# More of a modulation's weights loaded ahead, norms in another order, weight units freed earlier, and a branch in other PSUM banks

## The chip, the cores and the metric

The kernel runs on one core of a Trainium2 chip. The metric is the device time of one execution in microseconds (us). A core has five engines that run side by side, each through its own queue in order: TensorE (PE, matrix products; its loads of the fixed operand are PEld), VectorE (DVE), ScalarE (ACT), GpSimd (POOL) and SyncE (SP, which here only issues DMAs). Products are accumulated in banks of PSUM; all else lies in SBUF.

## What is computed

Two blocks, one behind the other, over 256 tokens of width 1024. The first has two layers of a mixer (four branches with gates) and a feed-forward, dense in layer 0 and a mixture of eight experts in layer 1, each behind a layer norm. The second has two layers of attention (two kinds side by side) and a dense feed-forward; its RMS norms and residuals are modulated by rows that come from the conditioning vector `c` through `w_mod`.

```python
def first_block(x, ...):
    for layer in range(DEPTH):                       # DEPTH = 2
        y = mixer_block(x, w_in[layer], ..., w_branch[layer], w_out[layer])
        x = layer_norm(DN_ALPHA * x + y, ln_g[layer, 0], ln_b[layer, 0])
        j = layer // 2
        if layer % 2 == 0:
            y = swiglu(x, ffn_w1[j], ffn_w3[j], ffn_w2[j])
        else:
            y = moe_ffn(x, router_w[j], router_b[j], exp_w1[j], exp_w3[j], exp_w2[j])
        x = layer_norm(DN_ALPHA * x + y, ln_g[layer, 1], ln_b[layer, 1])
    return x

def mixer_block(x, ...):
    ...
    merged = jnp.zeros_like(x)
    for i, (o, w) in enumerate(zip((o_swa, o_rwkv, o_fox, o_dsa), w_rows)):
        merged = merged + gates[:, :, i] * (o @ w)
    return merged @ w_out

def second_block(x, c, ...):
    cond = jax.nn.silu(c)
    for l in range(DEPTH):
        mod = (cond @ w_mod[l] + b_mod[l])[:, None, :]
        sh_a, sc_a, g_a, sh_f, sc_f, g_f = jnp.split(mod, N_MOD, axis=-1)      # N_MOD = 6
        h = rms_norm(x, norm_mix[l]) * (1 + sc_a) + sh_a
        ...                                                                    # attention of h: o_m, o_d
        x = x + g_a * (jnp.concatenate([o_m, o_d], axis=-1) @ w_out[l])
        h = rms_norm(x, norm_ffn[l]) * (1 + sc_f) + sh_f
        x = x + g_f * ((jax.nn.silu(h @ w_gate[l]) * (h @ w_up[l])) @ w_down[l])
    return x
```

## The kernel before

**Products in three parts.** Every large product of f32 operands is made of three PE products of rounded operands: each operand is split into a rounded part (`h`) and the remainder (`l`), and hh, hl and lh are added in PSUM. For weights the class `Stream` does it: `load` issues the DMA of a unit (512 KB, `raw`, L107 on SP) as soon as a `raw` buffer is free (four until the experts, nine from there), `pump` rounds the next unit on ScalarE (`wh`, L125) and emits the remainder of the unit before it on DVE (`wl`, L114). There are six pairs of `wh` and `wl` (`WB`); `W.done()` tells that PE's products with the units taken so far stand in the program, so that their pairs may be used again.

**Who sets the order.** The program is written out by hand, engine by engine, at build time. The main line (stages such as `gates1`, `branch1`, `w_out`, `ln`, `ffn`, `ffn2`, `rms`, `in_2`, each begun by `phase`) emits PE's products and calls `tick` between them; `tick` pumps the weight stream and lets side work (generators: attention chains, the modulation) emit its next piece, when a planner inside the program holds it to be ready by its own costs.

**The modulation** (`mods`) is side work from the first mixer to the second block. The matrix is 2 x 1024 x 6144; each of 24 rows of 512 columns is made of eight steps: SP loads 128 x 512 weights (256 KB, L1694), ScalarE scales them by `c` (L1709), POOL adds them up (L1711, seven of eight); then ScalarE rounds the sum (L1726), POOL makes its remainder (L1728), two PE products with ones add over the partitions, and the row goes to DRAM (L1737). The steps run in the stages that `MODS_IN` names alone. Between a scaling and the next, `ahead` keeps two loads under way (three for some columns), all from one pool of 41 tiles, `b2`.

**Feed-forward** (`ffn`, used three times: once in the first block, twice in the second). 2816 hidden columns in eleven pairs of 128. A pair `p` has 96 PE products of 256 columns for gate and up (in `sm` banks) and 24 of 512 for down (`ffn_down`, into four `acc` banks that stay to the end); down runs one pair behind, and the last two together.

**Projection** (`out_proj`): 96 products of 512 columns into four `acc` banks, for w_out of the mixers and of the second block. Weight units are taken one by one and the last `tail` of them at once, so that the first half of the tokens (t = 0) ends before the second.

**Passage** (`normed_T`): behind a projection or feed-forward, the residual, a norm (`part`, `stats`, `scale`, `shift`: DVE, with one step on POOL) and the transposes of both halves on PE; ScalarE copies the rounded part (`hi`) out of PSUM and DVE the remainder (`lows`, L744 and L750). With `mid`, PE begins the next product on the first half (`nat_start`).

**A mixer's branches**: in the order of `PLAN`, gates and branches; a branch's products go column by column to an `acc` bank, DVE multiplies with the gate (L935) and adds (L936), and in the last branch ScalarE rounds the sum (L940) and DVE makes its remainder (L941) for w_out. Both PSUM rings, `acc` and `sm`, have four banks.

## Time and profile before

| | |
|---|---|
| median of 3 runs (lowest to highest) | 2003.49 us (2001.23 to 2015.73) |
| the profiled execution | 2003.65 us, its span 2001.8 us |
| PE busy | 1832.4 us, 92% of the span |
| PEld, DVE, ACT, POOL busy | 81%, 72%, 58%, 23% |
| mean granted TensorE clock | 0.960 of full speed |
| DMA | 440.08 MB, 220 GB/s on the mean |

The span is the time from the first to the last instruction; outside it lie 1.85 us. Matmuls overlap and their ends are modelled, so a busy PE is not PE at its peak; stages are best compared with a stage that does the same products. The granted clock is the share of full speed (2.4 GHz) that the chip allowed; it is 1.0 or, at 1.2 GHz, 0.5, and a value between is a mean over a stretch.

### The profile page before, as it was taken

To read this page: it belongs to the slowest core of one execution; us is meant where nothing else is said; L and a number is where in the kernel's file an instruction comes from. 1 tells how busy PE (TensorE), PEld (TensorE's weight loads), DVE (VectorE), ACT (ScalarE), POOL (GpSimd) and SP (SyncE) were. 2 spreads that over 40 slices of the span, in tenths; PEclk is the share of its full clock that TensorE was granted. 3 is DMA by queue.
4 is the path that set the end of the run, shared out by engine and by line. 5 is a ranking of instruction groups with operands and counts; after the bars stand their busy time and mean duration, and the time that the engine had idled before them with its cause. 6 is when DMAs were issued, how large, how long until landed. Compare 5 with 4: busy or idle time off the path is not lost. (4 is left out here: it accounts for less than half of the span.)

```text
span 2001.8 us, 31995 instructions
## 1 busy us (share of the span) xinstructions
PE 1832.4 (92%) x11703; PEld 1625.0 (81%) x11703; DVE 1446.5 (72%) x2255; ACT 1170.8 (58%) x1875; POOL 468.0 (23%) x345
## 2 busy tenths in 40 slices
PE   7999987998899999799999999598799888978998
PEld 7899977987698999588888888486698876768998
DVE  5886776666688656788888888777566758857554
ACT  4465744666465564377777777366466655746443
POOL 0110252777530100100000000111246765113000
PEclk9999988999999999889999999798899998989999
DMA  7553575787864444679999999655378785436662
GB/s 218 152 155 106 173 250 186 261 278 243 268 179 140 136 127 137 208 237 334 365 326 352 327 353 354 233 190 161 76 267 281 253 305 191 148 126 210 196 194 95
DMA packets 287071, 440.08 MB, mean 220 GB/s; under 512 B 31764, under 2 KB 178304, under 8 KB 286904
## 3 DMA queue, kind: packets, MB, share of 16 engines
q1 hardware_dynamic: 281960, 428.29, 64.6%
q0 software_dynamic: 2912, 8.59, 1.6%
q8 instruction: 94, 1.54, 0.3%
q10 hardware_dynamic: 2032, 1.06, 0.2%
q14 instruction: 73, 0.60, 0.1%
HBM read 427.60 MB, written 9.75 MB: 218 GB/s over the span
## 5 line engine op out<-in xcount | busy, mean ns | idle before, releaser
L114 DVE TENSOR_TENSOR wl<-raw,wh 128x1024 fp32r<-128x1024 f32 (+2 forms) x694 | 875.9, 1303 | 175.5 <-ACT wh L125 170.5
L125 ACT CAST wh<-raw 128x1024 fp32r<-128x1024 f32 (+2 forms) x694 | 695.4, 1030 | 201.4 <-PE sm L336 61.0
L336 PE MATMUL acc<-wh,b 128*128 128x512 f32 (+1 forms) x1232 | 417.2, 408 | 22.3 <-DVE b L935 10.5
L336 PE MATMUL sm<-b,wh 128*128 128x256 f32 x2112 | 378.1, 283 | 0.9 <-ACT wh L125 0.9
L336 PE MATMUL acc<-b,wh 128*128 128x256 f32 x2048 | 368.2, 283 | 0.2 <-DVE b L416 0.2
L1711 POOL TENSOR_TENSOR b<-b,b 128x512 f32<-128x512 f32 x168 | 309.8, 1844 | 228.5 <-ACT b L1709 215.5
L336 PE MATMUL sm<-wh,b 128*128 128x512 f32 (+1 forms) x1120 | 342.0, 382 | 0.0
L336 PE MATMUL sm<-b,wl 128*128 128x256 f32 x1056 | 302.2, 286 | 38.2 <-DVE wl L114 38.2
L336 PEld LDWEIGHTS sm<-b,wh 128*128 128x128 f32 x2112 | 332.1, 194 | 4.8 <-ACT wh L125 1.4
L336 PEld LDWEIGHTS acc<-b,wh 128*128 128x128 f32 x2048 | 312.5, 189 | 8.7 <-issue 7.3
L336 PEld LDWEIGHTS acc<-wh,b 128*128 128x128 f32 x1232 | 240.5, 196 | 82.2 <-DVE b L935 13.6
L336 PE MATMUL acc<-b,wl 128*128 128x256 f32 x1024 | 286.1, 279 | 3.0 <-DVE wl L114 3.0
L336 PE MATMUL acc<-wl,b 128*128 128x512 f32 (+1 forms) x616 | 248.6, 404 | 4.3 <-DVE wl L114 4.3
L336 PEld LDWEIGHTS sm<-b,wl 128*128 128x128 f32 x1056 | 205.4, 195 | 44.7 <-DVE wl L114 44.6
L336 PEld LDWEIGHTS sm<-wh,b 128*128 128x128 f32 x1120 | 209.8, 189 | 35.0 <-issue 0.2
L1709 ACT ACTIVATE b<-b,ccol 128x512 f32<-128x512 f32 x192 | 137.4, 724 | 151.8 <-DMA b<-in_w_mod_dram 151.8
L336 PE MATMUL sm<-wl,b 128*128 128x512 f32 (+1 forms) x560 | 213.5, 381 | 0.0
L336 PEld LDWEIGHTS acc<-b,wl 128*128 128x128 f32 x1024 | 193.5, 189 | 3.6 <-DVE wl L114 3.6
L336 PEld LDWEIGHTS acc<-wl,b 128*128 128x128 f32 x616 | 120.8, 196 | 30.5 <-DVE wl L114 7.5
L553 POOL TENSOR_TENSOR ln_mv<-ln_mv,mhalf 128x1 f32<-128x1 f32 x8 | 7.5, 932 | 525.4 <-DVE ln_mv L664 525.4
L336 PEld LDWEIGHTS sm<-wl,b 128*128 128x128 f32 x560 | 105.9, 189 | 18.2 <-DVE wl L114 0.5
L340 PE MATMUL sm<-ident,b 128*128 128x128 f32 (+1 forms) x242 | 46.9, 339 | 72.6 <-DVE b L691 32.1
(333 smaller groups left out, 1738.7 us busy)
## 6 DMA issues: line engine op xcount, KB each, us to landing
raw<-in_exp_w_dram SPq DMA_DIRECT2D x216, 512.0 KB
raw<-in_w_in_dram SPq DMA_DIRECT2D x152, 512.0 KB
b<-in_w_mod_dram SPq DMA_DIRECT2D x192, 256.0 KB
raw<-in_ffn_w_dram SPq DMA_DIRECT2D x66, 512.0 KB
raw<-in_exp_w_dram SPq DMA_DIRECT2D x64, 384.0 KB
raw<-in_w_gate_dram SPq DMA_DIRECT2D x44, 512.0 KB
raw<-in_w_up_dram SPq DMA_DIRECT2D x44, 512.0 KB
raw<-in_w_down_dram SPq DMA_DIRECT2D x44, 512.0 KB
```

What stands on the lines that cost most here:

```text
L114: self.K.nc.vector.tensor_sub(*self.lows.pop())
L125: nc.scalar.copy(wh[:, :w], raw[:, :w])
L336: return self.nc.tensor.matmul(out, lhsT, rhs, start=start, stop=stop)
L340: r = self.nc.tensor.transpose(out, in_, ident)
L553: self.nc.gpsimd.tensor_tensor(ap, ap, self.mhalf[:, :n], op=OP.pow)
L1709: nc.scalar.activation(r, r, AF.Copy, scale=cc[:, k : k + 1])
L1711: nc.gpsimd.tensor_add(w["a"], w["a"], r)
```

## The change

**Loads of the modulation.** `MODS_IN` becomes a table of depths: `ahead` keeps as many loads under way as the running stage has there, 9 in the feed-forwards, and `steps` calls it more often. From three pairs before a feed-forward's end the depth is 2 again.

**Units freed ahead.** In `out_proj` and at the end of `ffn`, `W.dn` is moved on and a unit pumped before the last products; the mixers' `tail` is 4 instead of 5.

**Last branch.** Branch 1, the last of a mixer, takes `sm` banks, and the remainder for a column (L941, now L949) is emitted behind the next column's two operations.

**Passages.** `turn` is split into the transposes and `high`; the norm's steps of both halves come ahead of the transposes, the remainders last; the early product `mid` comes behind the second half's `shift`, and at r = 0 there is none.

```diff
-MODS_IN = ("branch3", "gates1", "branch0", "branch1", "w_out", "ffn", "ffn2")
+MODS_IN = {"branch3": 2, "gates1": 2, "branch0": 3, "branch1": 3, "w_out": 4, "ffn": 9, "ffn2": 9}
@@ def phase
         self.main = name
+        self.ahead = MODS_IN.get(name, 2)
@@ def out_proj
-    def out_proj(self, aT, nk, tail=5, split_at=None):
+    def out_proj(self, aT, nk, tail=4, split_at=None):
...
                 if t == 0:
                     self.tick()
+                elif j == tail - 3:
+                    self.W.dn = self.W.ti - 2
+                    self.W.pump()
@@ def normed_T
         if norm:
             part, stats, scale, shift = norm
-            for n in range(2):
-                part(0, n)
-                if early:
-                    scale(0, n)
-            stats(0)
+            for t in range(NT):
+                for n in range(2):
+                    part(t, n)
+                    if early and not t:
+                        scale(t, n)
+                if early and t:
+                    for n in range(2):
+                        scale(t, n)
+                stats(t)
+                if not early:
+                    for n in range(2):
+                        scale(t, n)
+                if not early and t == 0:
+                    for n in range(2):
+                        shift(t, n)
             if early:
-                part(1, 0)
-            else:
                 for n in range(2):
-                    scale(0, n)
-            for n in range(2):
-                shift(0, n)
-        self.turn(xT, src[0], 0, lows[0])
-        if mid:
-            rest = mid(xT)
-        if norm:
-            if early:
-                scale(1, 0)
-            else:
-                part(1, 0)
-            part(1, 1)
...
-        for o in lows[0]:
-            nc.vector.tensor_sub(*o)
+                    shift(0, n)
+        self.high(xT, self.turn(src[0]), 0, lows)
         if norm:
             for n in range(2):
                 shift(1, n)
-        self.turn(xT, src[1], 1, lows[1])
-        for o in lows[1]:
+        if mid:
+            rest = mid(xT)
+        self.high(xT, self.turn(src[1]), 1, lows)
+        for o in lows:
             nc.vector.tensor_sub(*o)
@@ def mixer
-                ps = self.acc().rearrange("p (a b) -> p a b", a=2)
+                ps = (self.acc() if nb < 4 else self.sm()).rearrange("p (a b) -> p a b", a=2)
...
                     nc.scalar.mul(mh[c], mt[c], 0.5)
-                    nc.vector.scalar_tensor_tensor(ml[c], mt[c], 0.5, mh[c], op0=OP.mult, op1=OP.subtract)
-                    del mt[c]
+                    if last:
+                        last()
+
+                    def last(c=c, m=mt.pop(c)):
+                        nc.vector.scalar_tensor_tensor(ml[c], m, 0.5, mh[c], op0=OP.mult, op1=OP.subtract)
@@ def ffn
+            if p == np_ - 3:
+                self.ahead = 2
...
         self.ffn_down(y, hid.pop(np_ - 2), ws[:2], False, False)
+        self.W.dn = self.W.ti - 2
+        self.W.pump()
         self.ffn_down(y, hid.pop(np_ - 1), ws[2:], False, False, True)
@@ def mods
-            while order and len(raws) < (3 if order[0][2] > 2 else 2) and not (self.hold and order[0][2] == 0):
+            while order and len(raws) < self.ahead and not (self.hold and order[0][2] == 0):
...
                 if not raws:
                     ahead()
                     yield AUTO
+                    ahead()
@@ def build
-                xT = self.normed_T(hs, norm, True, self.nat_start(512) if half == 0 else None)
+                xT = self.normed_T(hs, norm, True, self.nat_start(512) if r == 6 else None)
```

How the instructions stand now, at three places. Rows are in program order on one engine; a tile's last number tells buffers apart.

*Second feed-forward, the middle.* SP's loads before, of weights (`raw`) and modulation (`b` from `in_w_mod_dram`):

```order
L107 DMA raw_19622<-in_w_up_dram 128x4x256
L107 DMA raw_19640<-in_w_up_dram 128x4x256
L1694 DMA b_4380_19644<-in_w_mod_dram 128x512
L107 DMA raw_19676<-in_w_down_dram 128x1024
L107 DMA raw_19695<-in_w_down_dram 128x1024
L1694 DMA b_4389_19699<-in_w_mod_dram 128x512
L1694 DMA b_4390_19715<-in_w_mod_dram 128x512
L107 DMA raw_19727<-in_w_gate_dram 128x4x256
L1720 DMA b_4394_19729<-in_b_mod_dram 1x512
L107 DMA raw_19748<-in_w_gate_dram 128x4x256
L1694 DMA b_4399_19751<-in_w_mod_dram 128x512
L1694 DMA b_4400_19753<-in_w_mod_dram 128x512
```

and where ScalarE uses them: L1709 scales, L125 rounds a weight unit.

```order
L1709 ACTIVATE b_4399_19751<-b_4399_19751,ccol_425 128x512
L1333 ACTIVATE b_4406_19805<-sm_19731 128x512
L125 CAST wh_19820<-raw_19573 128x1024
L1726 CAST b_4411_19826<-b_4335_19384 128x512
L1709 ACTIVATE b_4400_19753<-b_4400_19753,ccol_425 128x512
L125 CAST wh_19869<-raw_19622 128x1024
L1709 ACTIVATE b_4401_19769<-b_4401_19769,ccol_425 128x512
```

The load of `b_4400` stands eleven rows behind that of `raw_19622`, and both are used side by side. SP's rows of the change at the same place:

```order
L107 DMA raw_19571<-in_w_gate_dram 128x4x256
L107 DMA raw_19595<-in_w_gate_dram 128x4x256
L1708 DMA b_4385_19610<-in_w_mod_dram 128x512
L1708 DMA b_4386_19626<-in_w_mod_dram 128x512
L107 DMA raw_19644<-in_w_up_dram 128x4x256
L1708 DMA b_4390_19648<-in_w_mod_dram 128x512
L107 DMA raw_19669<-in_w_up_dram 128x4x256
L1708 DMA b_4396_19685<-in_w_mod_dram 128x512
```

and ScalarE's:

```order
L1725 ACTIVATE b_4385_19610<-b_4385_19610,ccol_425 128x512
L125 CAST wh_19809<-raw_19529 128x1024
L1725 ACTIVATE b_4386_19626<-b_4386_19626,ccol_425 128x512
L1725 ACTIVATE b_4390_19648<-b_4390_19648,ccol_425 128x512
L125 CAST wh_19859<-raw_19571 128x1024
L1725 ACTIVATE b_4396_19685<-b_4396_19685,ccol_425 128x512
```

Here `b_4390` is used next to `raw_19571`, and its load stands five rows behind that one's.

*First feed-forward, the beginning.* SP's rows before, where the weights of the second pair and the constants of the next layer (`rows`) are loaded:

```order
L107 DMA raw_3733<-in_ffn_w_dram 128x4x256
L107 DMA raw_3756<-in_ffn_w_dram 128x4x256
L1694 DMA b_695_3763<-in_w_mod_dram 128x512
L1694 DMA b_696_3767<-in_w_mod_dram 128x512
L1737 DMA mod_223<-b_625_3448 1x512
L510 DMA rows_3774<-in_rwkv_mu_dram 8x128
L510 DMA rows_3774<-in_rwkv_w_dram 2x128
L510 DMA rows_3774<-in_rwkv_a_dram 2x128
```

and of the change:

```order
L107 DMA raw_3769<-in_ffn_w_dram 128x4x256
L1708 DMA b_700_3773<-in_w_mod_dram 128x512
L1708 DMA b_701_3775<-in_w_mod_dram 128x512
L1708 DMA b_702_3777<-in_w_mod_dram 128x512
L1708 DMA b_703_3779<-in_w_mod_dram 128x512
L1708 DMA b_704_3781<-in_w_mod_dram 128x512
L1708 DMA b_705_3783<-in_w_mod_dram 128x512
L1708 DMA b_706_3787<-in_w_mod_dram 128x512
L1753 DMA mod_223<-b_621_3427 1x512
L511 DMA rows_3794<-in_rwkv_mu_dram 8x128
L511 DMA rows_3794<-in_rwkv_w_dram 2x128
L511 DMA rows_3794<-in_rwkv_a_dram 2x128
```

Seven loads of the modulation stand in a row now, where two did.

*Layer 0, from the last branch to w_out.* DVE's rows before: L935 and L936 of a column, L941 its remainder, L114 weights:

```order
L935 SCALAR_TENSOR_TENSOR b_550_2970<-b_550_2970,acc_3371 128x512
L936 TENSOR_TENSOR b_393_2144<-b_393_2144,b_550_2970 128x512
L941 SCALAR_TENSOR_TENSOR b_613_3397<-b_393_2144,b_612_3396 128x512
L114 TENSOR_TENSOR wl_3385<-raw_3253,wh_3384 128x1024
L935 SCALAR_TENSOR_TENSOR b_562_3049<-b_562_3049,acc_3400 128x512
L936 TENSOR_TENSOR b_402_2186<-b_402_2186,b_562_3049 128x512
L941 SCALAR_TENSOR_TENSOR b_620_3426<-b_402_2186,b_619_3425 128x512
L114 TENSOR_TENSOR wl_3414<-raw_3293,wh_3413 128x1024
L935 SCALAR_TENSOR_TENSOR b_579_3155<-b_579_3155,acc_3429 128x512
```

and of the change (L939, L940 and L949 are the same operations):

```order
L939 SCALAR_TENSOR_TENSOR b_550_2972<-b_550_2972,sm_3377 128x512
L940 TENSOR_TENSOR b_395_2148<-b_395_2148,b_550_2972 128x512
L114 TENSOR_TENSOR wl_3391<-raw_3226,wh_3390 128x1024
L939 SCALAR_TENSOR_TENSOR b_566_3076<-b_566_3076,sm_3405 128x512
L940 TENSOR_TENSOR b_404_2190<-b_404_2190,b_566_3076 128x512
L949 SCALAR_TENSOR_TENSOR b_615_3403<-b_395_2148,b_614_3402 128x512
L114 TENSOR_TENSOR wl_3419<-raw_3264,wh_3418 128x1024
L939 SCALAR_TENSOR_TENSOR b_577_3151<-b_577_3151,sm_3435 128x512
L940 TENSOR_TENSOR b_408_2210<-b_408_2210,b_577_3151 128x512
L949 SCALAR_TENSOR_TENSOR b_623_3432<-b_404_2190,b_622_3431 128x512
```

The columns come out of `sm` banks, and a column's remainder stands behind the next column's two operations.

## Rows read from the trace of the kernel before

**Rows 1.** Stages, all engines: stretch, its length, busy us (instructions), clock, DMA share, GB/s.
```profile
312.00:538.60 226.60, 203.76 (x1347) 184.19 (x1345) 144.00 (x149) 136.41 (x186) 150.06 (x79) 0.93 0.79 260
1443.10:1661.40 218.30, 195.39 (x1331) 176.62 (x1330) 145.37 (x118) 132.79 (x180) 133.66 (x77) 0.97 0.81 267
1814.10:1996.70 182.60, 181.81 (x1322) 170.11 (x1320) 103.25 (x101) 85.25 (x99) 13.46 (x8) 0.99 0.58 183
```

**Rows 2.** Waits of ACT, 313 to 537: total us, times, longest us.
```profile
ACT b L1709 <- DMA b<-in_w_mod_dram: 62.5, 25, 6.2
```

**Rows 3.** Waits of ACT, 1443.1 to 1661.4.
```profile
ACT b L1709 <- DMA b<-in_w_mod_dram: 76.5, 24, 6.7
```

**Rows 4.** First feed-forward by pair, L1709 alone: stretch, length, ACT busy (scalings), clock, DMA.
```profile
312.00:349.50 37.50, 4.23 (x6) 0.79 0.67 214
...
382.80:399.90 17.10, 5.79 (x8) 1.00 0.76 261
...
418.00:440.50 22.50, 5.77 (x8) 0.92 0.73 243
...
503.50:521.10 17.60, 5.07 (x7) 1.00 1.00 347
521.10:538.60 17.50, 3.61 (x5) 0.90 0.83 247
```

**Rows 5.** The same of the second feed-forward.
```profile
1443.10:1469.60 26.50, 3.61 (x5) 0.92 0.86 248
...
1561.40:1584.60 23.20, 5.78 (x9) 0.93 0.80 265
1584.60:1601.50 16.90, 5.82 (x8) 1.00 0.85 283
...
1642.20:1661.40 19.20, 2.89 (x4) 0.82 0.74 267
```

**Rows 6.** The same of the third: its start, a pair, the last two down products.
```profile
1814.10:1837.60 23.50, 5.69 (x8) 0.96 0.73 243
...
1854.50:1870.90 16.40, 0.00 (x0) 1.00 0.63 196
...
1985.70:1996.70 11.00, 0.00 (x0) 1.00 0.10 40
```

**Rows 7.** Waits of SP's DMA queue, 312 to 538.6.
```profile
SPq L107 <- DVE wl L114: 112.1, 46, 17.4
```

**Rows 8.** DVE by line and shape, 1837 to 1990: busy us, mean ns, idle before.
```profile
L114 DVE TENSOR_TENSOR wl<-raw,wh 128x1024 fp32r<-128x1024 f32 x56 | 68.5, 1242 | 35.1 <-ACT wh L125 34.3
L416 DVE TENSOR_TENSOR b<-b,b 128x512 fp32r<-128x512 f32 x9 | 6.2, 693 | 6.4 <-ACT b L415 6.4
```

**Rows 9.** DVE by line and shape, 349.5 to 521.
```profile
L114 DVE TENSOR_TENSOR wl<-raw,wh 128x1024 fp32r<-128x1024 f32 x53 | 87.0, 1674 | 33.4 <-ACT wh L125 33.4
```

**Rows 10.** Timeline of DVE and POOL, 429 to 442: start, us, instruction.
```profile
429.30 1.27 POOL L1711 TENSOR_TENSOR b<-b,b 128x512 f32<-128x512 f32 x1 [0.79 <-ACT b L1709]
...
431.04 6.72 DVE L114 TENSOR_TENSOR wl<-raw,wh 128x1024 fp32r<-128x1024 f32 x3
...
432.21 8.94 POOL L1711 TENSOR_TENSOR b<-b,b 128x512 f32<-128x512 f32 x4
```

**Rows 11.** Waits of PE, 255 to 312.
```profile
PE acc L336 <- DVE b L935: 5.6, 3, 3.3
```

**Rows 12.** The two output projections of the mixers, all engines, columns of rows 1.
```profile
271.40:305.70 34.30, 27.18 (x100) 19.86 (x100) 25.19 (x31) 14.18 (x19) 12.83 (x8) 0.85 0.74 245
803.90:836.30 32.40, 26.68 (x103) 19.65 (x101) 21.50 (x31) 8.48 (x12) 0.99 (x1) 0.89 0.74 260
```

**Rows 13.** Waits of PE, the whole span.
```profile
PE sm L340 <- DVE b L691: 32.1, 8, 13.1
PE sm L340 <- DVE b L671: 14.6, 4, 5.0
```

**Rows 14.** Timeline of the passage behind w_out of layer 0.
```profile
309.01 1.41 DVE L744 TENSOR_TENSOR b<-sm,b 128x256 fp32r<-128x256 f32 x4
```

More of the change, by code (lines that the diff above doesn't have):

```diff
@@ L693, in rms_norm, with turn, high @@
         return part, stats, scale, shift
[L695 removed]
+    def turn(self, x):
+        r = []
+        for g in range(2):
+            r.append(self.sm().rearrange("p (a b) -> p a b", a=4))
+            for j in range(4):
+                self.tr(r[g][:, j], x[g][:, j * P : (j + 1) * P], self.ident)
+        return r
+    def high(self, xT, pss, t, lows):
         sl = (slice(None), slice(None), slice(t * P, (t + 1) * P))
[L698 to L701 removed]
+        for g, ps in enumerate(pss):
             for a in range(2):
@@ L1707, in steps @@
                     yield AUTO
+                    ahead()
                 r = raws.pop(0)
```

32 lines of the change are left out of this document (10 added, 22 removed).

## The prediction

> **What bounds the kernel now.** I read the busy time of the three dense feed-forward stages first, since they do the same products. The first runs from 312.0 to 538.6 us, the second from 1443.1 to 1661.4, the third from 1814.1 to 1996.7: 226.6, 218.3 and 182.6 us for the same PE work [rows 1]. The reader should see what differs: in the third, POOL works 13.46 us, in the others 150 and 134, because only those two also prepare the modulation. So 44.0 and 35.7 us are lost beside a stage that shows what PE can do.
>
> Then I asked what ScalarE waits for. In the first stage it stands 62.5 us in 25 waits before the modulation's scaling (L1709), for the DMA of the 256 KB that it scales [rows 2]; in the second 76.5 us in 24 waits [rows 3]. ScalarE also rounds every weight (L125) in the same queue. DVE makes the remainder (L114) only behind that rounding, and PE needs both: a late modulation load holds back weights that had long landed.
>
> Third, the stages by hidden pair, cut where PE goes from the gate and up products to the down products. A pair without modulation takes 16.4 us [rows 6]. With it the nine windows from 349.5 to 521.1 take 171.6 us, 19.1 on the mean [rows 4], and nine from 1469.6 to 1642.2 take 172.6 [rows 5]. But pairs with 8 scalings also ran in 17.1 us (382.8) and 16.9 us (1584.6) [rows 4, 5], so 8 a pair is possible; others took 22.5 and 23.2. In slow ones the granted clock reads 0.92 or 0.93 where fast ones read 1.00: part of each stall is spent at the lower of PE's two levels.
>
> Fourth, the two output projections of the mixers and the passages between stages (below).
>
> **Modulation loads ahead.** `MODS_IN` now gives each stage a depth: 9 in the feed-forwards, 2 to 4 before them; it was 2, or 3 for shift rows. In the order, a load stands a median 28 PE instructions ahead of its use before and 108 after; at 16.4 us for a pair's 120 matmuls that is 3.8 and 14.8 us (an estimate). Bytes and operations are the same, 192 loads and scalings; only their places move: 78 to 87 scalings in the first feed-forward, 75 to 80 in the second, 8 to none in the third, 5 to none in the projection of its layer. If the waits go, the nine middle windows of each stage fall towards a floor, and its size decides.
> One bound is PE: 16.9 us, the fast pair with 8 scalings. The other comes from DVE and POOL. L114 takes 1.242 us where POOL is idle [rows 8] and 1.674 where it works [rows 9]. From 431 to 441 three of them took 6.72 us and, beside them, four POOL additions 8.94 [rows 10]; one addition that met little took 1.27. End to end they would take 3 x 1.242 + 4 x 1.27 = 8.8 us: they ran one after the other. Were that always so, a pair with six L114, one L416 (0.693 [rows 8]) and eight POOL operations needs 7.45 + 0.69 + 10.16 = 18.3 us.
> The Trainium skill says the same outright ("SBUF — State Buffer", section "SBUF: two separate sides"): a DVE operation with two SBUF inputs and a GpSimd operation hold their shared ports for a whole instruction and the other blocks. By it the pair is 18.3 us; here 17.1 and 16.9 us were seen too, with fewer weights rounded in those windows, so the trace agrees in the pairs that it shows side by side.
> I take 17.7 for the mean, nearer the two rows than the 18.3, because POOL can fall behind for a while without holding PE. 9 x 17.7 = 159.3 gives 171.6 - 159.3 = 12.3 us in the first stage and 13.3 in the second. Bounds over both: 16.9 gives 14.4 us more, 18.3 gives 10.8 less.
>
> **Units freed ahead of a projection's end.** With `W.dn = W.ti - 2` and a `pump` in the last half of a projection, two more weight units are rounded there (L125 in the first w_out: 5 before, 7 after) and the tail holds four units instead of five. This moves ScalarE and DVE work under matmuls that are still running. The first feed-forward's start takes 37.5 us against 23.5 in the third [rows 4, 6]; its first products wait for L114. But in the order seven modulation loads now stand in a row ahead of the constants and the next weights on SP: 1.8 MB at the 265 to 347 GB/s of these windows [rows 4, 5], 5 to 7 us in front of weights needed soon. I book 3 us of the 14.0, between none and 14. The second's start has 26.5 against 23.5 and less to win: nothing.
> Ends: 17.5 and 19.2 us against 11.0 [rows 4 to 6]. In the first, the depth falls back to 2 from pair 8, so waits can return: 1.5 us. In the second no modulation is left at the end: 6 us, with the clock of 0.82 there. The third loses its 8 scalings: 1 us. Together 11.5, between 0 and 30.
>
> **The last branch in other banks.** The projection behind it needs four `acc` banks. Before, these are what branch 1 has just filled, and each is freed by DVE's L935; PE waits 5.6 us there, 3.3 in one piece [rows 11]. 96 matmuls of 512 columns cost 22.0 us (the 48 of the third stage's end take 11.0 [rows 6]); they took 34.3 us, and 32.4 in layer 1 with 7 matmuls more, at clocks of 0.85 and 0.89 [rows 12]. After, branch 1 fills `sm` banks, so the first product waits only for `mh[0]` and `ml[0]`; and L941 moves behind the next column's pair, so DVE no longer stands before ScalarE's result in each column. What is late next is `ml[0]`: it comes behind two columns' DVE work (about 4 us), which the other columns' matmuls mostly cover. I take 5.6 less 1 for that wait, plus 3 of the time lost at the lower clock: 7.5 us, and 5 in layer 1. Bounds: nothing (if `mh` and `ml` set the pace for every pair of rows) to 12.3 + 9.6 = 21.9.
>
> **Passages in another order.** PE waits 32.1 us for L691 and 14.6 for L671, the last step before each normed tile is transposed [rows 13]. In `normed_T` the four remainders of the first half (1.41 us [rows 14]) stood on DVE between the second half's statistics and that step; they now come last. The early product reads the rounded part alone and the router's and feed-forward's products start with it, so 1.4 us in each of three layer norms: 4 us. In the RMS passages (early = True) the first half's L691 moves behind the second half's work and takes the place that the remainders left: nothing. Dropping the early product at r = 0 adds 8 matmuls, 1.8 us, after the passage, but takes two roundings out of its middle: nothing. Bounds: 8 us won, 4 lost.
>
> **Sum.** 12.3 + 13.3 + 11.5 + 12.5 + 4 = 53.6 us off the profiled execution's 2003.65: 1950.0 us. The median of the runs is 2003.49, so the same holds for it.
>
> **Rivals.**
> *The ports hold the pairs (0.20).* Every pair takes 18.3 us, POOL is late, and ScalarE's rounding of the finished sum (L1726, now L1742) waits for it in front of the weights. 1950.0 + 10.8 = 1961 us. For it: rows 10. Against: 17.1 and 16.9.
> That is the rule of the Trainium skill's "SBUF — State Buffer", "SBUF: two separate sides", worked out above.
> *It doesn't do what it says (0.20).* The loads are earlier in the program, but SP's one queue stands 112.1 us before L107 for a free weight buffer, up to 17.4 us in one piece [rows 7], longer than the estimated 14.8 of lead. Half of the waits stay: half of 25.6 and of the 11.5 is lost, 1950.0 + 18.6 = 1969, and 1987 if all stay. Against: most of its 46 blocks are short (mean 2.4 us).
> *Slower (0.06).* In the first stage there are four weight buffers only. If the deeper modulation queue pushes each of 66 weight units behind one more load of 256 KB (0.99 us at 265 GB/s [rows 5]), and PE sees all of it, that costs 65 us; with the 41.3 us of the other terms it is 2003.65 + 65 - 41 = 2028. It decides from 0.92 us a unit on (61 us). Against: once full, the queue takes one load for each one used, as before; a window with 347 GB/s ran in 17.6 us [rows 4].
> *All waits go and PE sets the pace (0.05).* 1950.0 - 14.4 - 9.4 = 1926 us.
> *The gains are given back (0.04)*, mostly by weights rounded later in the planner's order: about 2000 us.
>
> **How the numbers follow.** The forecast itself has 0.45, at 1937 to 1962. The range of 8 in 10 runs from 1930, between it and the case where PE sets the pace, to 1982, between the two ends of the case of waits that stay. About 1% is what a measurement of this kernel can tell from none: below 1983.5 is faster, above 2023.5 slower. Half of the second rival lies above 1983.5. Faster: 0.45 + 0.20 + 0.10 + 0.05 = 0.80; same: 0.10 + 0.04 = 0.14; slower: 0.06.
>
> **What would show it.** ScalarE's waits for the modulation's DMA fall from 62.5 and 76.5 us to under 15 each, and windows of a pair lie at 17 to 18.3 us; if they lie at 20 with these waits gone, weights or ports hold them, and L114's mean (1.67 before) or waits for DMA on L125 tell which. The third feed-forward should stay within 2 us of 182.6. At the output projections no wait for L935 should remain, and 34.3 and 32.4 us become about 27. I am wrong if the waits stay with SP behind L107, if ScalarE waits over 20 us for POOL, or if a new wait for `mh` or `ml` takes the place of the banks'.

## The result, and the profile after

The changed kernel takes 1944.32 us (median of 4 runs, 1940.56 to 1945.73), the kernel before 2009.61 beside it; the ratio is 0.9685, 95% interval 0.965 to 0.972. It leaves out one slow run of the kernel before (2111.68 us), which the median of 2009.61 still holds. The forecast was 1950.0 us, 1930 to 1982. The profiled execution took 1945.73 us with a span of 1943.9, against 2003.65 and 2001.8 before: 57.9 us less, where the sum said 53.6.

| | before | after |
|---|---|---|
| PE busy | 1832.4 us, 92% | 1811.2 us, 93% |
| DVE, ACT, POOL busy | 72%, 58%, 23% | 76%, 60%, 24% |
| mean granted clock | 0.960 | 0.964 |
| DMA | 220 GB/s | 226 GB/s |

The same stages as in [rows 1], cut at the first product and the last (before, the first was cut 0.8 us ahead of the first product, the second and third 1.4 and 0.6 us behind it). Columns: stretch, length, PE, PEld, DVE, ACT, POOL busy us (instructions), clock, DMA share, GB/s.

```profile
312.00:521.80 209.80, 197.44 (x1345) 179.74 (x1344) 158.71 (x149) 141.62 (x194) 168.01 (x88) 0.95 0.85 287
1417.10:1605.20 188.10, 186.32 (x1340) 171.70 (x1338) 167.58 (x121) 136.70 (x188) 157.18 (x86) 1.00 0.93 313
1758.50:1939.20 180.70, 180.65 (x1322) 169.47 (x1320) 97.06 (x100) 79.30 (x90) 0.00 (x0) 1.00 0.55 174
```

About 225.8, 219.7 and 183.2 us have become 209.8, 188.1 and 180.7. The second feed-forward now carries the modulation and is only 7.4 us longer than the third, which has none. The first still loses 29.

What ScalarE waits for (total us, times, longest us), from 310 to 522 us and from 1414 to 1605, as [rows 2, 3] did:

```profile
ACT wh L125 <- DMA raw<-in_ffn_w_dram: 24.8, 24, 3.3
ACT b L1742 <- POOL b L1727: 17.0, 7, 5.5
ACT b L1725 <- DMA b<-in_w_mod_dram: 8.0, 3, 4.6
...
ACT b L416 <- DVE b L1346: 19.9, 10, 3.9
ACT b L1742 <- POOL b L1727: 19.1, 6, 6.9
```

The waits of 62.5 and 76.5 us for the modulation's DMA are 8.0 and none. Two others are new in size: the rounding of a finished sum (L1742) for POOL's last addition, and in the first stage the weights' own DMA (24.8 us in 24 pieces). In the second, ScalarE now also waits 19.9 us for DVE's product of gate and up (L1346; 2.3 before): DVE is busy for 167.6 of the 188.1 us. SP stands as long as before for a free weight buffer:

```profile
SPq L107 <- DVE wl L114: 108.8, 43, 15.0
```

against 112.1 in [rows 7]. By pair (columns of [rows 4]: ACT busy with L1725 alone, its count, clock, DMA):

```profile
343.60:360.00 16.40, 5.69 (x9) 1.00 0.85 280
...
445.30:462.10 16.80, 6.15 (x9) 1.00 0.96 332
462.10:481.90 19.80, 6.15 (x9) 1.00 0.71 243
481.90:503.30 21.40, 4.93 (x7) 0.92 0.93 325
503.30:521.80 18.50, 2.89 (x4) 0.82 0.72 207
...
1439.30:1455.70 16.40, 7.38 (x11) 1.00 1.01 353
...
1540.00:1558.70 18.70, 6.15 (x9) 1.00 0.70 238
...
1594.10:1605.20 11.10, 0.00 (x0) 1.00 0.87 301
```

A pair with nine scalings now usually takes 16.8 to 16.9 us, one with eleven 16.4. The difference is not in the scalings but in PE's own work: where a sum is finished, PE makes two products for its row (`onesr`), and that adds 0.47 us. PE, PEld and DVE busy (count) with this operand alone, for a window without the two products and one with them:

```profile
343.40:359.80 16.40, 0.00 (x0) 0.00 (x0) 0.00 (x0) 1.00 0.84 278
...
445.20:462.10 16.90, 0.63 (x2) 0.17 (x2) 0.00 (x0) 1.00 0.97 332
```

So an undisturbed pair is 16.4 us, and 0.47 more for each row that is finished in it. By this the nine windows of the first stage, with ten rows, would take 152.3 us and those of the second, with nine, 151.8 (an estimate); they took 159.7 and 154.8. Only the last three windows of the first stage and single ones of the second are clearly longer.

PE's waits at the second projection (777 to 815 us) and at the first feed-forward's start (312 to 344):

```profile
PE acc L336 <- DVE wl L114: 6.1, 1, 6.1
PE acc L336 <- DVE b L949: 0.9, 1, 0.9
...
PE sm L340 <- DMA rows<-in_gate_bias_dram: 3.4, 1, 3.4
```

No wait for the gate product (L939, before L935, [rows 11]) is left, but a wait of 6.1 us for a weight stands in layer 1 that was not there, and one of 3.4 us for the next layer's constants.

### The profile page after: what moved, and what is told of

It reads as the page before. It is cut to its first block, busy times and chain, and to the rows that moved or that the text cites. A ratio compares the mean times of both kernels' runs of the same rounds, so it can differ in the third digit from the quotient of the medians.

```text
span 1943.9 us, 32015 instructions
## 1 busy us (share of the span) xinstructions
PE 1811.2 (93%) x11703; PEld 1617.3 (83%) x11703; DVE 1472.4 (76%) x2255; ACT 1170.2 (60%) x1875; POOL 471.4 (24%) x345
## 5 line engine op out<-in xcount | busy, mean ns | idle before, releaser
L114 DVE TENSOR_TENSOR wl<-raw,wh 128x1024 fp32r<-128x1024 f32 (+2 forms) x694 | 899.6, 1338 | 118.2 <-ACT wh L125 111.8
L125 ACT CAST wh<-raw 128x1024 fp32r<-128x1024 f32 (+2 forms) x694 | 695.3, 1029 | 261.8 <-PE sm L336 71.6
L336 PE MATMUL acc<-wh,b 128*128 128x512 f32 (+1 forms) x1232 | 410.3, 404 | 12.7 <-ACT wh L125 5.5
L336 PE MATMUL acc<-b,wh 128*128 128x256 f32 x1984 | 359.1, 284 | 0.2 <-DVE b L417 0.2
L336 PEld LDWEIGHTS acc<-b,wh 128*128 128x128 f32 x1984 | 304.8, 190 | 8.5 <-issue 7.0
L336 PE MATMUL acc<-b,wl 128*128 128x256 f32 x992 | 278.0, 280 | 2.7 <-DVE wl L114 2.7
L336 PEld LDWEIGHTS sm<-wh,b 128*128 128x128 f32 x1120 | 209.5, 189 | 35.0 <-issue 0.2
L336 PEld LDWEIGHTS acc<-b,wl 128*128 128x128 f32 x992 | 188.4, 190 | 3.1 <-DVE wl L114 3.1
L1725 ACT ACTIVATE b<-b,ccol 128x512 f32<-128x512 f32 x192 | 131.8, 717 | 18.8 <-DMA b<-in_w_mod_dram 18.7
L336 PEld LDWEIGHTS sm<-wl,b 128*128 128x128 f32 x560 | 105.6, 189 | 17.6
L340 PE MATMUL sm<-ident,b 128*128 128x128 f32 (+1 forms) x242 | 48.0, 351 | 72.3 <-DVE b L695 29.7
```

The lines of the kernel that those rows point to most:

```text
L114: self.K.nc.vector.tensor_sub(*self.lows.pop())
L125: nc.scalar.copy(wh[:, :w], raw[:, :w])
L336: return self.nc.tensor.matmul(out, lhsT, rhs, start=start, stop=stop)
L340: r = self.nc.tensor.transpose(out, in_, ident)
L1725: nc.scalar.activation(r, r, AF.Copy, scale=cc[:, k : k + 1])
```

## The experiments

Each kernel was timed beside the kernel before on its chip. I compare ratios: 0.001 is 2.0 us, and the changed kernel's own 0.9685 is uncertain by 0.0035, so differences under some 8 us are read from the profiles, and those come from one execution each. The table gives, for each, where the time lies: from the first branch-1 product to the first layer-norm transpose (layers 0 and 1), and the two feed-forwards with modulation as start (first product to the first down product), nine middle windows, and end (to the last down product), in us from each trace's PE instructions.

| kernel | ratio | projection 0, 1 | first feed-forward | second |
|---|---|---|---|---|
| before | 1 | 40.6, 37.5 | 36.6 + 171.6 + 17.6 | 27.8 + 172.6 + 19.4 |
| changed | 0.9685 | 36.4, 37.0 | 31.3 + 159.7 + 18.5 | 22.0 + 154.8 + 11.2 |
| no_loads | 0.9893 | 37.4, 35.7 | 30.4 + 173.5 + 16.2 | 21.9 + 172.2 + 20.3 |
| no_units | 0.9696 | 35.1, 36.3 | 33.1 + 160.8 + 15.2 | 23.9 + 156.7 + 11.4 |
| no_banks | 0.9743 | 39.9, 37.6 | 35.8 + 154.8 + 22.9 | 22.9 + 155.2 + 11.2 |
| no_norms | 0.9731 | 37.2, 36.9 | 31.9 + 157.1 + 19.0 | 23.0 + 156.7 + 11.2 |
| keep_depth | 0.9661 | 36.8, 36.2 | 30.4 + 159.1 + 12.7 | 21.9 + 153.7 + 11.2 |
| late_round | 0.9627 | 37.1, 35.2 | 31.3 + 156.2 + 14.2 | 23.0 + 157.0 + 11.6 |
| router_early | 0.9643 | 36.9, 31.4 | 31.2 + 158.6 + 19.3 | 22.9 + 154.9 + 11.2 |
| tail5 | 0.9658 | 35.5, 34.9 | 33.2 + 158.6 + 18.8 | 23.0 + 154.9 + 11.2 |
| no_adds | 0.9715 | 39.4, 36.6 | 40.8 + 153.4 + 24.5 | 22.8 + 149.0 + 11.2 |
| consts_first | 0.9678 | 37.2, 37.3 | 27.3 + 157.2 + 18.6 | 22.7 + 154.1 + 11.2 |
| five | 0.9659 | 35.4, 33.3 | 30.6 + 157.9 + 11.7 | 22.9 + 151.4 + 11.2 |
| four | 0.9638 | 35.9, 34.7 | 30.7 + 157.7 + 15.9 | 22.9 + 160.6 + 11.2 |

### Each part of the change undone

**no_loads**

```diff
-MODS_IN = {"branch3": 2, "gates1": 2, "branch0": 3, "branch1": 3, "w_out": 4, "ffn": 9, "ffn2": 9}
+MODS_IN = ("branch3", "gates1", "branch0", "branch1", "w_out", "ffn", "ffn2")
...
-            while order and len(raws) < self.ahead and not ...
+            while order and len(raws) < (3 if order[0][2] > 2 else 2) and not ...
```

The lines that set `ahead` in `phase` and in `ffn`, and the two added calls in `steps`, go too.

> The changed kernel with only the modulation's depths undone (two loads ahead, three for shift rows; the rest of the change stays). If the lead of the loads is what emptied the two feed-forwards, ScalarE waits for the modulation's DMA for over 50 us in each again, the nine middle windows go back from 159.7 and 154.8 us to about 170 each, and the time is about 1944 + 27 (windows) + 8 (starts and ends) = 1979 us. Rival, that units freed ahead and the new order of the passages did it: under 1955 us, windows still under 162.

1984.15 us, ratio 0.9893 (0.9873 to 0.9913): 42 us lost. ScalarE's waits, 309 to 531 and 1420 to 1648 us:

```profile
ACT b L1720 <- DMA b<-in_w_mod_dram: 64.6, 24, 5.9
...
ACT b L1720 <- DMA b<-in_w_mod_dram: 75.3, 29, 8.4
```

L1720 is the scaling here. The waits are back at their old size, the middle windows at 173.5 and 172.2 us. The lead of the loads did this; SP stood for a free weight buffer in all three kernels, 108.8 to 127.4 us in the first stage.

**no_units**

```diff
-    def out_proj(self, aT, nk, tail=4, split_at=None):
+    def out_proj(self, aT, nk, tail=5, split_at=None):
-                elif j == tail - 3:
-                    self.W.dn = self.W.ti - 2
-                    self.W.pump()
@@ def ffn
-        self.W.dn = self.W.ti - 2
-        self.W.pump()
```

> The changed kernel with the units freed ahead undone: tail 5 again in the mixers' projections, no extra unit rounded before a projection's or a feed-forward's last products. By the prediction's term (3 us at the first feed-forward's start, part of the ends): 1947 to 1950 us. Rival, that the shorter tail costs as much at the passage behind w_out as it gives (24 products instead of 30 behind which the first half's norm is worked, 1.4 us each): 1942 to 1945 us, with the passage from w_out to the first feed-forward's products under 7.3 us.

1946.72 us, ratio 0.9696 (0.9681 to 0.971): 2 us, not to be told from none. The shorter tail does both: w_out of layer 0 and the norm behind it are 2.8 us shorter without it, the feed-forward behind starts 1.8 slower. The second feed-forward's start is 1.9 us longer, with a wait of 1.6 us for L114 that the changed kernel has not. The third feed-forward is 6.4 us longer here: 2.7 at its start, where PE waits 1.4 us for L114, and 3.8 in the middle without any wait, where each block of 96 gate and up products takes 11.47 us instead of 11.07 (see the last section).

**no_banks**

```diff
-                ps = (self.acc() if nb < 4 else self.sm()).rearrange("p (a b) -> p a b", a=2)
+                ps = self.acc().rearrange("p (a b) -> p a b", a=2)
...
-                    if last:
-                        last()
-
-                    def last(c=c, m=mt.pop(c)):
-                        nc.vector.scalar_tensor_tensor(ml[c], m, 0.5, mh[c], op0=OP.mult, op1=OP.subtract)
+                    nc.vector.scalar_tensor_tensor(ml[c], mt[c], 0.5, mh[c], op0=OP.mult, op1=OP.subtract)
+                    del mt[c]
```

> The changed kernel with the last branch in acc banks again and each column's remainder right behind its rounding. By the prediction (7.5 and 5 us): about 1956 us, with PE waiting 5 to 6 us for the gate product's bank in each layer. By the two traces the changed kernel gained 4.2 us from branch 1 to the layer norm in layer 0 and 0.5 us in layer 1, where a wait of 6.1 us for a weight's remainder took the place; then about 1949 us, and in layer 1 the wait for the weight is shorter while the bank's is back.

1956.18 us, ratio 0.9743 (0.9729 to 0.9756): 12 us, the size of the prediction. PE's waits at the two projections (266 to 308 and 785 to 824 us; L938 is L935 of before):

```profile
PE acc L336 <- DVE b L938: 5.4, 3, 2.7
...
PE acc L336 <- DVE b L938: 5.6, 3, 2.9
```

The banks' wait is back in full. But at the projections only 3.5 and 0.6 us are lost; 4 lie in the first feed-forward (213.5 against 209.5 us) and 1 to 2 each in later stages. In the first feed-forward the loss is at the start (35.8 against 31.3 us): PE stands 9.4 us for one weight's remainder, whose rounding is queued on ScalarE behind the sine of the rotary tables. For that sine ScalarE waits 6.7 us, where it was 2.9 in the changed kernel. PE's and ScalarE's waits, 314 to 351 us:

```profile
PE sm L336 <- DVE wl L114: 9.6, 2, 9.4
...
ACT sin L1784 <- DVE rp_a L1781: 6.7, 1, 6.7
```

So most of the 12 us is not the term of the prediction, though it has its size. The planner spread the modulation otherwise later on: 72 scalings in the second feed-forward instead of 80, 8 in the second mixer instead of 3. That this makes the rest is argued, not shown.

**no_norms**

```diff
-        self.high(xT, self.turn(src[0]), 0, lows)
-        if norm:
-            for n in range(2):
-                shift(1, n)
-        if mid:
-            rest = mid(xT)
-        self.high(xT, self.turn(src[1]), 1, lows)
-        for o in lows:
-            nc.vector.tensor_sub(*o)
+        self.turn(xT, src[0], 0, lows[0])
+        if mid:
+            rest = mid(xT)
+        ...
+        for o in lows[0]:
+            nc.vector.tensor_sub(*o)
+        if norm:
+            for n in range(2):
+                shift(1, n)
+        self.turn(xT, src[1], 1, lows[1])
+        for o in lows[1]:
+            nc.vector.tensor_sub(*o)
```

> The changed kernel with the old order of the passages (remainders between the halves, the early product behind the first half, also at r = 0). By the prediction (1.4 us in each of three layer norms, nothing elsewhere): about 1948 us. Rival, that the RMS passages changed too (r = 0 took 12.4 us to its first product and 5.3 now, but its projection 75.3 and 79.5): a loss of 3 us more there, about 1951; or the early product at r = 0 was worth having: 1942.

1953.76 us, ratio 0.9731 (0.9718 to 0.9744): 9 us. From the profiles, the layer norms lose 1.3, 1.9 and 1.0 us (first transpose to the next stage's first product), 4.2 together, as predicted. The RMS passages have to be counted from the last product ahead of them, because the change itself begins their transposes later. So counted, the two ahead of the feed-forwards lose 1.2 and 1.3 us. The one at r = 0 loses 4.6 but its projection wins 4.4, and the one at r = 6 wins 2.4 (9.6 us against 12.0). Together that is 0.3, where nothing was booked. The starts of the second and third feed-forward lose another 1.0 and 1.7; the rest is spread over other stages.

The four losses add to 65 us and the whole change gives 63 (0.0315 of 2007). As far as four differences of ratios can tell, each uncertain by some 8 us, the parts hardly share anything.

### What still holds

**keep_depth**

```diff
-            if p == np_ - 3:
-                self.ahead = 2
```

> The changed kernel without the rule that lowers the depth to 2 from three pairs before a feed-forward's end. The first feed-forward's last three windows take 19.8, 21.4 and 18.5 us where 16.8 was seen before them; ScalarE waits there for the modulation's DMA 8.0 us in three pieces. If the fallen depth makes that, the stage goes from 210.5 to about 203 us and the time to about 1937 us. Rival, that the stretch is held by POOL's late sums (ScalarE waits 17.0 us for them) and by weights that come from four buffers (24.8 us of ScalarE's waits for their DMA): the same time within 3 us, or slower because the loads run on into the layer norm's passage.

1942.33 us, ratio 0.9661 (0.9634 to 0.9688). Both theories were half right. The end falls from 18.5 to 12.7 us, so the lowered depth made that; the two windows ahead of it stay. But most of this is given back at once: from the last product to the first of the next stage go 11.9 us instead of 7.7, since DVE still makes two weights' remainders (506.8 to 511.1 us) in front of the layer norm's first residual. 1.7 us are left at this place.

```profile
458.00:477.50 19.50, 17.66 (x122) 15.72 (x122) 15.10 (x12) 13.79 (x20) 19.11 (x10) 1.00 0.80 272
477.50:498.90 21.40, 19.20 (x127) 17.47 (x125) 13.73 (x10) 13.12 (x19) 20.85 (x12) 0.92 1.01 368
498.90:511.60 12.70, 12.16 (x50) 8.60 (x48) 10.63 (x10) 9.25 (x15) 12.31 (x8) 1.00 0.91 267
```

POOL is busy 19.1 of 19.5 us and 20.9 of 21.4 in these two.

**late_round**

```diff
+            yield 6000
             ah, al = self.b2((P, 512), F32R), self.b2((P, 512), F32R)
             nc.scalar.copy(ah, a)
```

> The changed kernel with one yield added: the rounding of a finished sum on ScalarE is emitted 6 us of the planner's time later. In the changed kernel ScalarE stands 17.0 and 19.1 us before it for POOL's last addition, with weights behind it in its queue (windows of 19.8, 21.4, 18.7 and 18.3 us). If that wait makes these windows: the waits fall under 5 us each and the time by 5 to 8 us, to about 1938. Rival, that POOL and DVE are simply full there, so that the weights' remainders are late whoever waits: the same time within 3 us.

1935.75 us, ratio 0.9627 (0.96 to 0.9654), by the ratios 12 us below the changed kernel's and the fastest of all, though the two intervals just touch. ScalarE's wait for POOL from 312 to 518 us falls from 17.0 us to

```profile
ACT b L1743 <- POOL b L1727: 4.4, 2, 2.4
```

and the first stage's last windows from 19.8, 21.4 and 18.5 us to 18.4, 19.7 and 14.2. In the second stage it is the other way: the wait grows to 22.7 us with one piece of 10.1, and the stage loses 3.6. Another 4 us come from the second mixer, where the planner set the order anew; that part is an accident. So the wait for late sums costs the first stage some 6 us (7.8 to its last product, of which the passage behind takes 2.1 back). In the second nothing was won by moving it; that POOL is simply full there, as the rival had it, fits this but is not shown.

**router_early**

```diff
-    def load_router(self):
+    def fetch_router(self):
...
+        self.router = raw, rb
+
+    def load_router(self):
+
+        raw, rb = self.router
...
+        self.fetch_router()
         ps = self.mixer(1, xT, begun, lc, L, lambda: (more(), self.load_router()))
```

> The changed kernel with the router's weights loaded before the second mixer instead of at its w_out; their rounding stays where it was. In the second w_out PE waits 6.1 us for a weight's remainder while ScalarE stands 7.7 us before the router's rounding for its DMA, which SP issued behind three blocked weights, and the clock falls to 1.2 GHz right behind it. If that wait ate the gain expected of the other banks in layer 1: w_out goes from 31.3 to about 24 us (22.0 is PE alone) and the time to about 1937. Rival, that w_out's own weights are late (ScalarE waits 3.0 us for their DMA): w_out stays over 29 us.

1939.0 us, ratio 0.9643 (0.9614 to 0.9672). The second w_out, columns of the stages above, in the changed kernel:

```profile
783.40:814.80 31.40, 24.38 (x99) 19.23 (x99) 21.14 (x30) 10.12 (x12) 0.99 (x1) 0.89 0.77 246
```

and with the router's weights loaded early:

```profile
780.50:806.20 25.70, 23.00 (x99) 17.74 (x97) 20.50 (x29) 10.05 (x13) 0.99 (x1) 1.00 0.88 288
```

5.7 us less, and the clock at full speed. In the changed kernel's timeline SP issues the router's weights at 790.27 us, behind weights that waited for a buffer, and ScalarE needs them for a rounding of 0.24 us with three weight units queued behind it:

```profile
790.27 1.00 SPq L1412 DMA_DIRECT2D rt_w<-in_router_w_dram  x1
...
797.59 0.24 ACT L416 CAST rt_wh<-rt_w 128x64 fp32r<-128x64 f32 x1 [7.72 <-DMA rt_w<-in_router_w_dram]
797.75 2.93 ACT L125 CAST wh<-raw 128x1024 fp32r<-128x1024 f32 x3
```

This wait existed before the change too (5.6 us on ScalarE) and cost PE little while PE stood for the banks (0.8 us for L114 there, 6.1 now). It became the next to be late.

**tail5**

```diff
-    def out_proj(self, aT, nk, tail=4, split_at=None):
+    def out_proj(self, aT, nk, tail=5, split_at=None):
```

> The changed kernel with the mixers' tail back at 5 units, all else kept (the extra units rounded before the last products too). With all units' edits undone, the stretch from w_out to the next products became 2.8 us shorter in layer 0 and 2.0 in layer 1, while the feed-forwards' ends became longer. If the shorter tail is what costs there (the first half's norm has 24 products to lie behind instead of 30), this gives about 1944 - 5 = 1939 us. Rival, that the unit rounded ahead makes the difference in the projections too: 1944.

1941.55 us, ratio 0.9658 (0.9631 to 0.9686). From w_out to the first product 3.2 us less in layer 0 and 2.9 in layer 1; the first feed-forward's start costs 1.9 more. With 24 products behind which the first half's norm is worked, DVE is not done with it in time: in the changed kernel the second half's last residual (L2128) starts at 306.52, 3.3 us behind w_out's last product, where the kernel before began it (L2112) at once. The unit rounded ahead at the feed-forwards' ends gives nothing that shows: middle and end of the first together take 177.4 us with it here, 176.0 without it in no_units.

**no_adds**

```diff
-                if k:
-                    nc.gpsimd.tensor_add(w["a"], w["a"], r)
-                else:
+                if not k:
                     w["a"] = r
```

> The changed kernel without POOL's additions of the modulation (seven of eight scaled blocks of each row are left out of its sum; loads, scalings, rounding, remainder and rows stay). If the shared use of SBUF by DVE and POOL sets the length of a pair, L114 goes from two lengths (1.2 and 2.3 us) to 1.2 and the pairs with modulation fall well below 16.8 us, towards the 16.4 of a pair without it, and the late windows too: 1944 - 20 or more. If PE sets it and POOL only holds back through the late sums, pairs stay at 16.4 to 16.9 us, the windows of 19.8, 21.4, 18.7 and 18.3 us fall to that, and the time to about 1932 us.

1947.9 us, ratio 0.9715 (0.9695 to 0.9735): not faster. Neither theory foresaw that. L114 in the first feed-forward's nine windows, changed kernel's first seven and then this one (busy us, mean ns, idle before):

```profile
L114 DVE TENSOR_TENSOR wl<-raw,wh 128x1024 fp32r<-128x1024 f32 x43 | 82.8, 1969 | 9.5 <-ACT wh L125 9.5
```

```profile
L114 DVE TENSOR_TENSOR wl<-raw,wh 128x1024 fp32r<-128x1024 f32 x51 | 62.1, 1230 | 33.8 <-ACT wh L125 33.8
```

and the nine windows themselves:

```profile
353.20:506.50 153.30, 153.26 (x1105) 141.26 (x1103) 83.85 (x86) 125.05 (x177) 17.32 (x13) 1.00 1.01 355
1443.90:1592.90 149.00, 149.00 (x1087) 139.47 (x1087) 80.18 (x77) 79.59 (x95) 5.18 (x3) 1.00 0.76 246
```

L114 takes 1.23 us instead of 1.97, yet a pair takes 153.3 / 9 = 17.0 us, where the changed kernel's undisturbed ones take 16.8: PE is busy for the whole of both. The 0.2 us are rows again: twelve are finished in these nine windows and three in those of the second stage, and 9 x 16.4 us with 0.47 for each row are 153.2 and 149.0, which is what both stages took. So the shared ports do not set an undisturbed pair. What the additions cost the changed kernel in these windows is then at most what it takes there above PE's own work, 7.4 and 3.0 us; late_round shows for the first stage that the late sums are a part of it. (The plain differences, 6.3 and 5.8, hold other numbers of rows; in the second stage no_adds has 24 scalings instead of 80.) It is given back, most likely because the planner, with POOL free, draws 119 scalings into the first feed-forward (87 before): there the DMA moves 355 GB/s at a share of 1.01, ScalarE waits 21.8 us for the modulation again, and the stage's start and end grow to 40.8 and 24.5 us.

**consts_first**

```diff
         lc = self.spawn(self.layer_consts(1, L), "consts")
+        self.advance(lc)
```

> The changed kernel with the next layer's constants (rows) loaded at the very start of the first feed-forward instead of behind seven loads of the modulation. In the changed kernel PE waits 3.4 us for these rows at 323.5 us, a wait that the kernel before does not have, and the clock is at 1.2 GHz for 6.8 us right behind it. If the deep queue makes this wait: the stage's first window falls from 31.4 us by 3.4 and some 2 to 3 of the clock's loss, the time to about 1938 us. Rival, that the rounding of the gate weights (ScalarE waits 5.3 us behind its own DMA issues and 2.9 for the angles of the rotary tables) sets the start anyway: the same time within 2 us.

1940.01 us, ratio 0.9678 (0.966 to 0.9697). The first feed-forward's start, in the changed kernel and here:

```profile
312.10:343.60 31.50, 27.38 (x198) 26.71 (x197) 18.74 (x47) 17.38 (x25) 6.76 (x5) 0.85 0.70 229
```

```profile
310.10:337.40 27.30, 24.25 (x197) 23.25 (x197) 17.90 (x48) 17.37 (x25) 7.73 (x5) 0.98 0.81 260
```

4.2 us less and the clock at 0.98 instead of 0.85: the wait was that of the rows behind seven loads. Taking the seven loads away helps less (30.4 us in no_loads), as PE then waits 4.7 us there for L114. The median shows 1.4 of the 4.2, inside its interval.

**five** and **four**

```diff
-    def out_proj(self, aT, nk, tail=4, split_at=None):
+    def out_proj(self, aT, nk, tail=5, split_at=None):
...
+            yield 6000
...
+        self.advance(lc)
...
+        self.fetch_router()
```

in both (the last with the split of `load_router` as in router_early), and in five also

```diff
-            if p == np_ - 3:
-                self.ahead = 2
```

> Five edits together on the changed kernel: the router's weights loaded before the second mixer, the tail of 5 units, the depth kept to the feed-forwards' ends, the rounding of a sum emitted 6 us later, the constants' rows loaded first. Alone, by their profiles' stages, the first gives 5.6 us (second w_out), the second 6 (w_out and the norms behind it), the third 6 (both feed-forwards), the fourth 6 in the first feed-forward and a loss of 3.6 in the second, the fifth 5 if its theory holds. If they add up: about 1944 - 25 = 1919 us. Rival, that edits in one stage overlap (third and fourth both shorten the first feed-forward's end): about 1927.

> The five edits without the kept depth. In the run of five, the second mixer took 4.9 us longer in branch 3 (13 scalings of the modulation fell into it instead of 3) and the first feed-forward 205.4 us where the later rounding alone had 204.2. If the kept depth spoiled those stages and the rest adds up: about 1936 (later rounding alone) - 5 (router) - 3 (tail in layer 0) = 1928 us, or 1924 with the constants' 4. Rival, that the edits overlap and the clock's low stretches move elsewhere: 1935 us, as with five.

1935.64 us, ratio 0.9659 (0.9636 to 0.9681), and 1938.09 us, 0.9638 (0.961 to 0.9665). The gains don't add up, and the reason that I gave for it (the kept depth) was wrong: four has the slow second mixer as well. Its branch 3 there:

```profile
718.90:741.50 22.60, 19.46 (x126) 16.44 (x123) 14.38 (x38) 14.66 (x38) 8.65 (x7) 0.77 0.32 103
```

against this of the changed kernel:

```profile
726.50:743.70 17.20, 15.16 (x125) 12.90 (x125) 12.58 (x40) 10.43 (x30) 1.02 (x1) 1.00 0.20 62
```

Seven scalings of a row that had been begun in the first feed-forward fall into it, and the clock is 0.77. In keep_depth and five eight fall there, and the clock stands at 1.2 GHz for 10.2 us as it does here. A row has eight, and must be finished before the experts: moving the feed-forward's end by a few us probably decides whether a part of a row is left over. In the second feed-forward four takes 160.6 us for the middle windows, where five has 151.4 with eight scalings fewer (64 against 72). No kernel was clearly faster than late_round alone.

## Why the prediction was right, and where its steps were not

The mechanisms were mostly right, but that the time lay so near the forecast is partly luck, since errors of both signs cancelled: middle windows 29.7 us (25.6 booked), starts and ends 20.9 (11.5), projections 4.7 (12.5), and the small rest of 2.6 in the passages and single stages (4).

**Loads ahead: right.** The waits went, as said, and the nine windows fell by 11.9 and 17.8 us (12.3 and 13.3 were booked); undone, they are worth 13.8 and 17.4. The rival with SP's queue fell: SP was blocked for 108.8 us and the waits went all the same, its longest block, 15.0 us, being about the 14.8 of lead estimated. The slower rival shows a trace only: ScalarE's wait for the first stage's weights grew from 7.3 to 24.8 us, in pieces of 1 us.

**The size of a pair: the step that failed.** I put the floor between 16.9 (PE) and 18.3 (DVE and POOL end to end) and took 17.7. The 17.7 came out as the first stage's mean (159.7 / 9), but not for the reason given: seven windows took 16.4 to 17.4 us and two 19.8 and 21.4. Where it fails is the price of a couple. From 1494 us on, DVE ran four L114 in a row and POOL five additions:

```profile
1493.11 9.72 POOL L1727 TENSOR_TENSOR b<-b,b 128x512 f32<-128x512 f32 x5
...
1494.88 9.04 DVE L114 TENSOR_TENSOR wl<-raw,wh 128x1024 fp32r<-128x1024 f32 x4
```

They do run in turns, but a turn of both takes 9.04 / 4 = 2.26 us, not 1.242 + 1.27 = 2.51. This price stood in [rows 10] already: three L114 in 6.72 us are 2.24 each. Six turns, an L417 of 1.68 (with its share of POOL) and one more addition of 1.27 make 16.5 us (an estimate): less than PE's 16.9. One of the two fast pairs that I set aside as having fewer weights rounded, that from 1584.6 us on, had seven L125 (and six L114), more than a pair needs, beside its eight scalings:

```profile
1584.60:1601.50 16.90, 7.02 (x7) 1.00 0.85 283
```

(ACT busy with L125 alone.) In it the weights' work of a pair and six POOL operations fit into 16.9 us, though POOL began only at 1588.9. And the 16.9 itself is 16.4 with one finished row, as the windows after and those of no_adds show. The Trainium skill ("SBUF — State Buffer", section "SBUF: two separate sides") calls the pair of ports an exclusive lock for a whole instruction; the two lengths of L114, 1.21 and 2.31 us, agree with it. The 18.3 us that I drew from it do not.

**The ports as a rival: true in another place.** Undisturbed pairs are not held by it, but POOL ends its sums late, and ScalarE stands in front of the weights for that, 17.0 and 19.1 us, as the rival had it; both lie just under the 20 that I had named as a sign of being wrong. It cost the first stage some 6 us by late_round and at most 7.4 in its nine windows by no_adds; in those of the second at most 3.0. The rival put 1.4 us above PE's 16.9 on every pair, 25 over both stages.

**Starts and ends: gains where said in part, sizes off.** 11.5 us were booked and 20.9 came: the starts gave 5.3 and 5.8 (3 and 0 booked), the ends -0.9 and 8.2 (1.5 and 6), the third stage as a whole 2.5 (1). The first stage's end is the fallen depth that I named, 5.8 us by keep_depth, of which the passage behind gives back 4.2. The units freed, for which the 3 us stood, give 1.8 at the first start and take 2.8 before it: nothing. That start lost 3.4 us to the constants behind seven loads; the order rows showed it and I counted only the weights behind them. The second start became 5.8 us shorter where I booked nothing. Before, from 1441.7 to 1469.4 us, PE waited 2.7 us there for weights, at a clock of 0.90:

```profile
PE sm L336 <- DVE wl L114: 2.7, 2, 2.0
```

Now it waits for nothing there, at a clock of 0.99. Of the parts undone, the units bring 1.9 us back, with a wait of 1.6 for L114, and the passages 1.0, at a clock of 0.95; the rest is open.

**Other banks: mechanism right, sizes off.** The wait for the banks went (5.6 and 4.9 us), a wait for `ml[0]` of 2.8 and 0.9 us took its place, 1 was booked. From branch 1 to the norm 4.2 us were won in layer 0 instead of 7.5, and 0.5 in layer 1 instead of 5, where the router's weights were late next. The stretches of [rows 12], for which I had said 27, take 28.5 and 31.4 us. I had asked what is late next on DVE alone; ScalarE's queue held the answer in the trace of before.

**Passages: layer norms right in size, RMS passages right in sum alone.** Undone, the layer norms lose 4.2 us for the 4 booked; beside the kernel before they are 2.9 shorter (-0.3, 2.9 and 0.3). In the RMS passages I booked nothing, and no_norms gives 0.3, but as a sum of gains and losses that I had not seen. I reasoned that the first half's L691 takes the place that the remainders left. It does, but both halves are now transposed in one run. In the passage behind the first attention's projection PE stood twice before, for 0.89 and 4.24 us; now

```profile
1413.88 3.59 PE L340 MATMUL sm<-ident,b 128*128 128x128 f32 x16 [3.54 <-DVE b L695]
```

once, and from the projection's last product to the next stage's first go 6.8 us instead of 8.0. At r = 6, where the early product stays, the later first half costs: PE now stands

```profile
1611.83 1.94 PE L340 MATMUL sm<-ident,b 128*128 128x128 f32 x8 [6.73 <-DVE b L695]
```

ahead of it, and the passage takes 12.0 us instead of 10.8.

## What to carry to other kernels

A load that an in-order engine waits for holds everything queued behind it: count, for each small operand, what stands ahead of its load and what stands behind its use. Removing a stall uncovers the next wait in the same queue, and it is often already in the trace, on another engine and harmless so far. Where a planner decides the order, an edit in one stage moves work to others, so effects of a few us from single edits don't add up. And count a stage up to the next stage's first product: an end that became 5.8 us shorter left 1.7 when the passage behind it was counted too.

## What was not expected of the hardware

DVE's subtractions (L114) and POOL's additions ran in turns at 2.26 us a couple, 0.25 less than their lengths alone, and in the undisturbed pairs the doubled length of DVE's operation cost PE nothing. The DMA reached 353 to 368 GB/s in the fullest windows (share 1.01); that this is the next limit of a stage that carries both weights and modulation was not tried. And in no_units the middle of the third feed-forward ran 3.6% slower in its 256-column products at the full clock and without a wait (281 ns instead of 276 for the mean product, 11.47 us instead of 11.07 for 96): what sets this pace was not found.
